# 29 blocks of seven products in a decoder layer's down projection, with sums of weights also made beside the down runs and in the output projection

## The chip, the core and the metric

One core of a Trainium2 chip runs one launch of the kernel. A core has TensorE (PE, matrix products into PSUM), VectorE (DVE), ScalarE (ACT), GpSimd (POOL) and SyncE (SP), which here only issues DMA transfers between DRAM and the core's SBUF. Each engine works through its own list of instructions in order, and they wait for each other on semaphores. The metric is the device time of one launch in microseconds, as a median of runs.

## What is computed

A decoder layer for 256 tokens of width 2048, in float32:

```python
h = rms_norm(x, attn_norm_g)
q, k, v, p = split(h @ w_in)                     # 1024 columns each
a = moba_attention(rms_norm(q), rms_norm(k), v, rel_bias)
m = multiscale_pool(p, pool_w, pool_scale)
x = x + concatenate([a, m]) @ w_out              # output projection, 2048 x 2048
h = rms_norm(x, ffn_norm_g)
u = causal_conv(h @ w_up)                        # up projection, 2048 x 11264
gate, val = split(u)
x = x + (silu(gate) * val) @ w_down              # down projection, 5632 x 2048
```

The change touches the down projection and what prepares it.

## The kernel before

**Three products for one.** A float32 operand is kept as a high part (rounded by ScalarE to a shorter format, `wh`) and a low part (the rest, `wl`, by VectorE). A product is the sum of three matmuls: high x high, high x low, low x high (`product`).

**Rows of weights.** All weights stream from DRAM in the order of use, as *rows* of 128 x 2048 floats (1 MB). For each row SP issues a load into a tile `raw` (`load`, L151), ScalarE makes the high part (`high`, L182), VectorE the low part (`low`, L188), TensorE multiplies. There are four `raw` tiles and, from the output projection on, a fifth; four tiles for high parts, three for low parts. They are used in turn. The low part's end releases the `raw` tile, and `release` then issues the next load of a fixed order. SP takes its loads in that order, so a load whose tile is not free yet holds up what stands behind it.

**Steps.** The program is a list of half rows, written out by one loop at the end of `layer`. At the half row u the loop writes: the high part of the row three ahead, the low part of the row two ahead, a sum of weights if one is due there (`make`), delayed work (`agenda`, filled by `later(n, f)`: n half rows on), deferred work (the folds), and then the matmuls of u. Each engine's order follows from this.

**Thirds and runs.** After the output projection the 22 hidden blocks of 256 are done in three *thirds* (8, 8 and 6 blocks). In each an up stage computes the hidden values, and then two down *runs* follow, one for each half of the 2048 output columns (`nb` 0 and 1). A run adds its blocks' products in PSUM and at its end adds that to the residual `x2`.

**Eights and sevens.** The product of a hidden block (2 tiles of tokens x 2 of hidden) with its weights (2 x 2 tiles, 512 columns wide) takes eight products: an *eight*, one row of kind "tok", 24 matmuls. A *seven* takes seven products after Strassen and Winograd, 21 matmuls, of sums of hidden tiles (`left_sums`) and sums of weight tiles. It needs two rows: a *sum* row (four tiles, among them three sums) with 12 matmuls, and a *rest* row (three tiles, 1536 columns) with 9. Which blocks of a run are sevens is told by `SEVEN`. Some of the products of a run's sevens are kept in PSUM banks of their own (`run["p"]`); after the last seven a *fold* (`seven_sums`: a copy by ScalarE, L918, and seven operations of VectorE, L919 to L926) brings them into the residual.

**Sums of weights.** The sums for a seven are made ahead, by one of two ways, and lie in DRAM (`mixed`) until their row is loaded. By `make`: the four tiles are loaded as a row, VectorE does three additions (L196 to L198), SP stores the result (L199). By `make_stage`: POOL issues four accumulating transfers. Before, 22 of the 26 are made by `make`, all in the up stages, and four by `make_stage`:

```python
SEVEN = ((1, 2, 3, 4, 5), (1, 2, 3, 4, 5), (1, 2, 3))
STAGES = (0, 2, 4, 6)
EARLY = (72, 72, 80, 80)
BY_DVE = ((2, 3, 4, 5, 6, 7), (0, 0.5, 1, 1.5, 2, 3, 4, 5, 6, 7), (0, 0.5, 1, 2, 3, 4))
```

**PSUM.** A run has eight banks of 512 columns: two pairs (`acc`, here `twos`) and four single ones (`ones_`). In the first run of a third the output gathers in the single ones (`c`) and the sevens' products in the pairs (`p`), in the second the other way round.

Of the kernel before, what the change touches and what calls it, by code (L numbers as in the profile page):

```python
# [26 lines left out]
OP = mybir.AluOpType  # L27
# [32 lines left out]
SOFF, SPAD = 32, 64  # L60
# [8 lines left out]
def plan():  # L69

    rows = [(k, i) for i, k in enumerate(24 * ["tok"] + 25 * ["feat"])]
    makes, t = [(u, None) for u in EARLY], 0
    for (g0, g1), sevens, by_dma, by_dve in zip(THIRDS, SEVEN, BY_DMA, BY_DVE):
        c = rows[-1][1] + 1
        makes += [(2 * c + u, None) for u in by_dma] + [(None, len(rows) + 4 * int(p) + (5 if p % 1 else 2)) for p in by_dve]
        rows += [("feat", c + i) for i in range(4 * (g1 - g0))]
        c = rows[-1][1] + 1
        for i in range(2 * (g1 - g0)):
            if i % (g1 - g0) in sevens:
                rows.append(("sum", t))  # L80
                t += 1
            rows.append(("rest" if i % (g1 - g0) in sevens else "tok", c + i))
    assert len(makes) == t, (len(makes), t)
    return rows, makes
# [12 lines left out]
def layer(ctx: ExitStack, tc: tile.TileContext, xT, wts, mix, mix12, par, rel_d, ident_d, icnt_d, out):  # L97
# [28 lines left out]
    order = [r for c in range(len(rows)) for r in [c] + [("make", i) for i, m in enumerate(makes) if m[1] == c]][4:]  # L126
# [74 lines left out]

    def make_stage(i, stage):

        t = mixed[i].rearrange("p (a n) -> p a n", n=512)
        if stage == 0:
            nc.gpsimd.dma_start(mixed[i], mix[i])
        elif stage == 1:
            nc.gpsimd.dma_start(t[:, :2], mix12[i][:, None, :].to_broadcast([P, 2, 512]), accum_op=OP.add)
        elif stage == 2:
            nc.gpsimd.dma_start(t[:, 2], t[:, 0], accum_op=OP.add)  # L210
        else:
            nc.gpsimd.dma_start(t[:, 3], t[:, 2], accum_op=OP.add)
# [391 lines left out]
    hold, splits, now, agenda, pending = set(), [], [0], {}, []  # L604
# [92 lines left out]
    def open_late():  # L697
        ectx.close()
        pool = ctx.enter_context(tc.tile_pool(name="late", bufs=1))
        late["pool"] = pool  # L700
        late["x2f"] = [block("x2f").rearrange("p (k t) -> p k t", t=S) for _ in range(4)]
# [13 lines left out]
    def block(name, dt=F32):  # L715
        return late["pool"].tile([P, SPAD + 1024], dt, name=name, tag="sums", bufs=5)[:, SOFF:SOFF + 1024]
# [39 lines left out]
    def sums2():  # L756
        sq, pool = late["sq"], late["pool"]
        x, r = sq[:, 1, :], pool.tile([P, 8], F32, name="prow", tag="prow")
        nc.vector.transpose(x, sq[:, 0, :])
        nc.vector.tensor_reduce(r, x.rearrange("p (j b) -> p j b", b=32), axis=AX.X, op=OP.add)  # L760
        q = pool.tile([32, 3, 8], F32, name="qrow", tag="qrow")
# [7 lines left out]
        late["row"] = pool.tile([P, S], F32, name="row", tag="row")  # L769
        nc.gpsimd.dma_start(late["row"], bass.AP(tensor=d.tensor, offset=d.offset, ap=[[0, P], [1, S]]))  # L770
# [92 lines left out]
    def left_sums(y):  # L863

        y = y.rearrange("p a (b n) -> p (a b) n", n=P)
        a11, a21, a12 = (y[:, i, :] for i in range(3))
        s = late["pool"].tile([P, 2, S], F32, name="ls", tag="ls").rearrange("p a (b n) -> p (a b) n", n=P)
        nc.vector.tensor_tensor(s[:, :2, :], y[:, 0:4:3, :], y[:, 1:2, :].to_broadcast([P, 2, P]), op=OP.subtract)
        nc.vector.tensor_tensor(s[:, 2, :], s[:, 1, :], a11, op=OP.add)
        nc.vector.tensor_tensor(s[:, 3, :], a12, s[:, 2, :], op=OP.subtract)  # L870
# [14 lines left out]
    def seven_mixed(u, j, run, first):  # L885

        c = where[u][0]
        t3, t1, t2, t4 = quarters(c)
        del wparts[c]
        s3, s1, s2 = (tuple(late["S", j][:, a, i, :] for a in range(2)) for i in range(3))  # L890
        a22 = tuple(late["hid"][:, 2 * j + 1, a, P:] for a in range(2))
        p1, p5, p6, p7 = run["p"]
        product(p5, s1, t1, first, False)
        product(p6, s2, t2, first, False)
        product(p7, s3, t3, first, False)
        product(run["c"][1][0], a22, t4, (1, 0) in run["left"], False)

    def seven_rest(u, j, run, first, last):
# [5 lines left out]
        s4 = tuple(late["S", j][:, a, 3, :] for a in range(2))  # L904
# [5 lines left out]
        if last:  # L910
            deferred.append(lambda: seven_sums(run))

    def seven_sums(run):

        x2, c = late["x2"], run["x2"]
        p1, p5, p6, p7 = run.pop("p")
        a, b, d = (scratch(n).rearrange("p a n -> p (a n)") for n in ("sa", "sb", "sa"))
        nc.scalar.activation(a, p1, AF.Copy)  # L918
        nc.vector.tensor_tensor(b, a, p6, op=OP.subtract)  # L919
# [6 lines left out]
        nc.vector.tensor_tensor(second, second, p5[:, None, :].to_broadcast([P, 2, 512]), op=OP.subtract)  # L926

# [25 lines left out]
    for n, ((g0, g1), sevens) in enumerate(zip(THIRDS, SEVEN)):  # L953
        ups = []
        for g in range(g0, g1):
            ups.append(feat_block(lambda: late["h"], XK, lambda ps, g=g: gate(ps, g)))
            ups.append(feat_block(lambda: late["h"], XK,
                                  lambda ps, g=g, j=g - g0, sevens=sevens, end=g == g1 - 1: value(ps, g, j, j in sevens, end)))
# [5 lines left out]
        for nb in range(2):  # L964
            run = {"n": nb * 1024}

            def done(t, lo, m, run=run, n=n, nb=nb):
# [10 lines left out]
                if n == 2:  # L978
                    k = min(m, 768 - lo) if nb and t else m
                    nc.sync.dma_start(out[:, t, run["n"] + lo:run["n"] + lo + k], x2[:, :k])  # L980
# [4 lines left out]
            for j in range(g1 - g0):  # L985
                def chunk(u, j=j, nb=nb, run=run, sevens=sevens, size=g1 - g0, fresh0=fresh0, end=n == 2 and nb == 1):
                    if j == 0:
# [17 lines left out]
                steps.append([lambda u, j=j, run=run, sevens=sevens: j in sevens and  # L1005
# [6 lines left out]
    for k, lag in enumerate(STAGES):  # L1012
        for i, (m, _) in enumerate(makes):
            if m is not None:
                agenda.setdefault(m + lag, []).append(lambda i=i, k=k: make_stage(i, k))
# [6 lines left out]
    for u in range(n):  # L1022
# [4 lines left out]
        elif u in starts:  # L1027
            c, now[0] = starts[u] + 2, u
            if c < FROM:
# [7 lines left out]
            for i, m in enumerate(makes):  # L1037
                if m[1] == c:
# [15 lines left out]
def chunks(w_in, pool_w, w_out, w_up, w_down):  # L1054
# [5 lines left out]
    (_, makes), mix, mix12 = plan(), [], []  # L1060

    def pair(w, k, c0, seven):
        b11, b12, b21, b22 = (w[(k + i) * P:(k + i + 1) * P, c0 + j * 512:c0 + (j + 1) * 512]
                              for i in range(2) for j in range(2))
        if seven:
            mix.append(np.concatenate([b22, *((b11, b11) if makes[len(mix)][1] is None else (b12, b11)), b21], axis=1))
            mix12.append(b12)
# [15 lines left out]
    for (g0, g1), sevens in zip(THIRDS, SEVEN):  # L1083
        for g in range(g0, g1):
            out += feat(w_up, 256 * g, XK) + feat(w_up, DFF + 256 * g, XK)
        for nb in range(2):
            for j in range(g1 - g0):
                out += pair(w_down, 2 * (g0 + j), 1024 * nb, j in sevens)
    return np.stack([np.concatenate(out[i:i + 2], axis=1) for i in range(0, len(out), 2)]), np.stack(mix), np.stack(mix12)
# [38 lines left out]
```

## Time and profile before

| | |
|---|---|
| median of 3 runs | 990.45 us (990.42 to 991.35) |
| the profiled execution | 990.44 us, its span 988.6 us |
| granted TensorE clock | 1.000 |
| TensorE, busy share of the span | 99%, 5282 matmuls |
| VectorE | 83%, 854 instructions |
| ScalarE | 62%, 719 instructions |
| GpSimd | 8%, 134 instructions |
| DMA | 285.34 MB, mean 289 GB/s |

The span runs from the first to the last instruction of one execution; the execution's own time has some 1.8 us around it. A group of instructions is printed as line, engine, operation, out<-in, partitions x elements and count, then busy time in us and the mean of one in ns, then the engine's idle time just before them and what ended it. A timeline's row has start and length in us, the engine, line and operation, and in brackets the idle time ahead of it and its releaser. Names in a row are those of the program's tiles.

### The profile page before, as it was taken

To read this page: it belongs to the slowest core of one execution; us is meant where nothing else is said; L and a number is where in the kernel's file an instruction comes from. 1 tells how busy PE (TensorE), PEld (TensorE's weight loads), DVE (VectorE), ACT (ScalarE), POOL (GpSimd) and SP (SyncE) were. 2 spreads that over 40 slices of the span, in tenths; PEclk is the share of its full clock that TensorE was granted. 3 is DMA by queue.
4 is the path that set the end of the run, shared out by engine and by line. 5 is a ranking of instruction groups with operands and counts; after the bars stand their busy time and mean duration, and the time that the engine had idled before them with its cause. 6 is when DMAs were issued, how large, how long until landed. Compare 5 with 4: busy or idle time off the path is not lost.

```text
span 988.6 us, 13485 instructions
## 1 busy us (share of the span) xinstructions
PE 983.5 (99%) x5282; PEld 851.7 (86%) x5282; DVE 816.5 (83%) x854; ACT 610.8 (62%) x719; POOL 74.6 (8%) x134
## 2 busy tenths in 40 slices
PE   9999999999999999999999999999999999999998
PEld 8888888898888888888888888888888888888887
DVE  6776859867678988998899888998888888898886
ACT  6654446456447767776755646886774646766742
POOL 0302322211112310000000000000000000000000
PEclk9999999999999999999999999999999999999999
DMA  9959775699978889676978788879687988776582
GB/s 349 317 207 305 248 242 202 208 330 367 297 206 305 275 335 351 259 294 230 390 259 336 297 338 334 343 296 341 231 313 291 380 290 336 287 305 255 191 326 79
DMA packets 49038, 285.34 MB, mean 289 GB/s; under 512 B 6712, under 2 KB 9400, under 8 KB 20496
## 3 DMA queue, kind: packets, MB, share of 16 engines
q1 hardware_dynamic: 41920, 264.17, 71.5%
q0 software_dynamic: 7056, 20.33, 7.7%
q8 instruction: 41, 0.67, 0.3%
q14 instruction: 21, 0.17, 0.0%
HBM read 253.14 MB, written 39.72 MB: 296 GB/s over the span
## 4 chain that ended last, share of the span: by engine, by line
PE 99%; DMA 0%; DVE 0%; SPq 0%; ACT 0%; issue 0%; DVEq 0%
PE ps_feat L276 41%; PE ps_down L879 22%; PE ps_feat L278 21%; PE ps_tok L264 9%; PE ps_val L254 4%; PE ps_pool L285 1%; PE ps_s L497 1%; DMA raw<-in_wts 0%; PE ps_av L533 0%; PE ps_av L535 0%; PE ps_val L245 0%; DVE x L977 0%; SPq L151 0%; ACT wh L159 0%; PE ps_feat L273 0%; PE ps_row L409 0%
## 5 line engine op out<-in xcount | busy, mean ns | idle before, releaser
L276 PE MATMUL ps_feat<-x2h,wh 128*128 128x512 f32 x1406 | 478.2, 389 | 0.0
L188 DVE TENSOR_TENSOR wl<-raw,wh 128x2048 fp32r<-128x2048 f32 (+1 forms) x171 | 375.6, 2204 | 25.9 <-ACT wh L182 8.0
L278 PE MATMUL ps_feat<-x2h,wl 128*128 128x256 f32 x1408 | 388.6, 276 | 0.0
L182 ACT ACTIVATE wh<-raw 128x2048 fp32r<-128x2048 f32 (+1 forms) x171 | 316.1, 1852 | 107.6 <-PE ps_down L879 55.9
L276 PEld LDWEIGHTS ps_feat<-x2h,wh 128*128 128x128 f32 x1406 | 263.9, 188 | 54.8
L278 PEld LDWEIGHTS ps_feat<-x2h,wl 128*128 128x128 f32 x1408 | 264.3, 188 | 0.0
L879 PE MATMUL ps_down<-wh,hid 128*128 128x512 f32 (+1 forms) x448 | 142.6, 387 | 0.0
L160 DVE TENSOR_TENSOR wl<-raw,wh 128x2048 fp32r<-128x2048 f32 (+3 forms) x44 | 82.9, 1894 | 37.7 <-ACT wh L159 29.5
L545 ACT ACTIVATE fs<-ps_feat 128x512 f32<-128x512 f32 x52 | 31.1, 598 | 133.5 <-PE ps_feat L278 117.4
L879 PEld LDWEIGHTS ps_down<-wh,hid 128*128 128x128 f32 x448 | 83.9, 188 | 17.3
L276 PE MATMUL ps_feat<-cat,wh 128*128 128x512 f32 x256 | 87.3, 389 | 0.0
L879 PE MATMUL ps_down<-wl,hid 128*128 128x512 f32 (+1 forms) x224 | 86.7, 387 | 0.0
L548 DVE TENSOR_TENSOR fs<-ps_feat,fs 128x512 f32<-128x512 f32 x52 | 35.8, 689 | 60.8 <-ACT fs L545 60.8
L264 PE MATMUL ps_tok<-wh,xh 128*128 128x512 f32 x256 | 80.1, 391 | 0.0
L813 ACT ACTIVATE z<-u,pv 128x256 f32<-128x256 f32 x176 | 79.1, 498 | 0.0
L159 ACT ACTIVATE wh<-raw 128x2048 fp32r<-128x2048 f32 (+3 forms) x44 | 69.3, 1598 | 10.5 <-DMA raw<-in_wts 7.6
L278 PE MATMUL ps_feat<-cat,wl 128*128 128x256 f32 x256 | 70.7, 276 | 0.0
L879 PE MATMUL ps_down<-wh,sums 128*128 128x512 f32 x208 | 69.2, 389 | 0.0
L819 DVE TENSOR_TENSOR y<-y,z 128x512 f32<-128x512 f32 x88 | 60.6, 688 | 9.2 <-ACT z L813 4.2
L276 PEld LDWEIGHTS ps_feat<-cat,wh 128*128 128x128 f32 x256 | 48.1, 188 | 10.0
L264 PEld LDWEIGHTS ps_tok<-wh,xh 128*128 128x128 f32 x256 | 48.1, 188 | 9.9
L811 ACT ACTIVATE y<-u,pv 128x256 f32<-128x256 f32 x88 | 51.8, 588 | 0.0
(190 smaller groups left out, 1013.7 us busy)
## 6 DMA issues: line engine op xcount, KB each, us to landing
raw<-in_wts SPq DMA_DIRECT2D x152, 1024.0 KB, 7.4
raw<-mixed SPq DMA_DIRECT2D x26, 1024.0 KB, 6.6
raw<-in_mix SPq DMA_DIRECT2D x22, 1024.0 KB, 6.8
mixed<-raw SPq DMA_DIRECT2D x22, 1024.0 KB, 6.5
raw<-in_wts SPq DMA_DIRECT2D x26, 768.0 KB, 5.5
raw<-in_wts SPq DMA_DIRECT2D x4, 512.0 KB, 7.1
mixed<-in_mix POOLq DMA_DIRECT2D x4, 512.0 KB, 16.8
mixed<-mixed POOLq DMA_DIRECT2D x8, 256.0 KB, 9.3
```

The costliest lines, as they stand in the source:

```text
L159: nc.scalar.activation(wh, w, AF.Copy)
L160: nc.vector.tensor_tensor(wl, w, wh.bitcast(F32), op=OP.subtract)
L182: nc.scalar.activation(w, raws[c][:, :width(c)], AF.Copy)
L188: nc.vector.tensor_tensor(wl, raws[c][:, :width(c)], wh.bitcast(F32), op=OP.subtract)
L254: nc.tensor.matmul(ps[b][:, t, :], xh[:, k, a, ts], w[:, ws], start=False, stop=(k == KT - 1 and n == 2), skip_group_check=True)
L264: nc.tensor.matmul(ps[:, t, :], act[:, k0 + k, a, ts], w[:, ws], start=(first and k == 0 and n == 0), stop=(last and k == 1 and n == 2))
L276: nc.tensor.matmul(ps, wh[:, ws], act[:, k, :, :], start=(bool(first) and n == 0), stop=False, skip_group_check=True)
L278: nc.tensor.matmul(ps[:, S:], wl[:, ws], act[:, k, 0, :], start=False, stop=(last and n == len(ks) - 1), skip_group_check=True)
L811: nc.scalar.activation(y[:, m, :], u[:, m, 2:], AF.Identity, scale=cw[2], bias=col(C_CB + f))
L813: nc.scalar.activation(z[i][:, m, :], u[:, m, 1 - i:1 - i + S], AF.Copy, scale=cw[1 - i])
L819: nc.vector.tensor_tensor(y, y, t, op=OP.add)
L879: nc.tensor.matmul(ps, a, w, start=(first and n == 0), stop=(last and n == 2), skip_group_check=True)
```

## The change

Five things change together.

- **More sevens.** `SEVEN` is now told per run: 5 and 5 in the first third, 6 and 6 in the second (5 and 5 before), 4 and 3 in the last (3 and 3 before): 29 in place of 26.
- **All 29 sums by VectorE.** `make_stage` and its array go. `EARLY` now names rows of the output projection (38, 40, 42, 44), behind whose low part a sum is made. 21 sums lie in the up stages. Four are made beside sevens: one in each run of the first two thirds, just behind the low part of the rest row of block 4 (`BESIDE`).
- **The fold in two parts.** ScalarE's copy is issued right behind the last seven's matmuls. VectorE does four of the seven operations then and three two half rows later (except at the program's end).
- **PSUM banks.** In the second run of a third the output gathers in one pair and two single banks, and the products in the other pair and the other single banks; in the first run the two pairs swap places.
- **The left sums** are made in place, by four operations of 128 columns in place of one of 256 and two of 128, and their low part is written out ahead of a row's low part (`firsts`). The output's stores of the first run of the last third come two half rows later. Tiles of the pool "late" are laid out anew.

```diff
-SEVEN = ((1, 2, 3, 4, 5), (1, 2, 3, 4, 5), (1, 2, 3))
-STAGES = (0, 2, 4, 6)
-EARLY = (72, 72, 80, 80)
-BY_DMA = ((), (), ())
-BY_DVE = ((2, 3, 4, 5, 6, 7), (0, 0.5, 1, 1.5, 2, 3, 4, 5, 6, 7), (0, 0.5, 1, 2, 3, 4))
+SEVEN = (2 * ((1, 2, 3, 4, 5),), 2 * ((1, 2, 3, 4, 5, 6),), ((1, 2, 3, 4), (1, 2, 3)))
+EARLY = (38, 40, 42, 44)
+PLACES = ((2, 3, 4, 5, 6, 7), (0, 0.5, 1, 1.5, 2, 3, 4, 5, 6, 7), (0, 0.5, 1, 2, 3))
+BESIDE = (4, 4, None)
...
+            if i % (g1 - g0) == beside:
+                makes.append(len(rows))
+            rows.append(("rest" if seven else "tok", c + i))
...
     def left_sums(y):
...
-        nc.vector.tensor_tensor(s[:, :2, :], y[:, 0:4:3, :], y[:, 1:2, :].to_broadcast([P, 2, P]), op=OP.subtract)
-        nc.vector.tensor_tensor(s[:, 2, :], s[:, 1, :], a11, op=OP.add)
-        nc.vector.tensor_tensor(s[:, 3, :], a12, s[:, 2, :], op=OP.subtract)
+        for out_, a, b, op in ((3, 3, 1, OP.subtract), (1, 0, 1, OP.subtract), (0, 3, 0, OP.add), (2, 2, 0, OP.subtract)):
+            nc.vector.tensor_tensor(s[:, out_, :], s[:, a, :], s[:, b, :], op=op)
         pending.append(lambda: nc.scalar.activation(parts[:, 0], s, AF.Copy))
-        later(4, lambda: nc.vector.tensor_tensor(parts[:, 1], s, parts[:, 0].bitcast(F32), op=OP.subtract))
+        firsts.setdefault(now[0] + 4, []).append(
+            lambda: nc.vector.tensor_tensor(parts[:, 1], s, parts[:, 0].bitcast(F32), op=OP.subtract))
...
         if last:
-            deferred.append(lambda: seven_sums(run))
+            a = scratch("sa").rearrange("p a n -> p (a n)")
+            nc.scalar.activation(a, run["p"][0], AF.Copy)
+            deferred.append(lambda: seven_sums(run, a))
...
-    def seven_sums(run):
+    def seven_sums(run, a):
...
         nc.vector.tensor_tensor(c(0, 0), a, c(0, 0), op=OP.add)
-        nc.vector.tensor_tensor(c(0, 1), c(0, 1), b, op=OP.subtract)
+        d = scratch("sd").rearrange("p a n -> p (a n)")
         nc.vector.tensor_tensor(d, b, p7, op=OP.add)
-        nc.vector.tensor_tensor(c(1, 0), d, c(1, 0), op=OP.add)
-        nc.vector.tensor_tensor(c(1, 1), c(1, 1), d, op=OP.subtract)
         second = x2[:, :, run["n"] + 512:run["n"] + 1024]
         nc.vector.tensor_tensor(second, second, p5[:, None, :].to_broadcast([P, 2, 512]), op=OP.subtract)
+
+        def rest():
+            nc.vector.tensor_tensor(c(0, 1), c(0, 1), b, op=OP.subtract)
+            nc.vector.tensor_tensor(c(1, 0), d, c(1, 0), op=OP.add)
+            nc.vector.tensor_tensor(c(1, 1), c(1, 1), d, op=OP.subtract)
+        if run["end"]:
+            rest()
+        else:
+            later(2, rest)
...
-                        run["c"], run["acc"], p = (twos, pair, ones_) if nb else (ones_, (None, None), twos)
-                        if end:
-                            run["c"], run["acc"], p = [twos[0], ones_[0]], (pair[0], None), [twos[1], ones_[1]]
-                        run["p"] = p[1][1], p[0][0], p[0][1], p[1][0]
-                        run["spare"] = p[1][1]
+                        if nb:
+                            run["c"], run["acc"], p = [twos[1], ones_[0]], (pair[1], None), [twos[0], ones_[1]]
+                        else:
+                            run["c"], run["acc"], p = ones_, (None, None), twos[::-1]
+                        run["p"] = p[0][0], p[1][1], p[0][1], p[1][0]
+                        run["spare"] = p[0][0]
```

What it moves is seen best in the engines' own lists. VectorE in the first run of the second third, from the rest row of block 4 on, before (1536 wide is a rest row, 2048 a sum row or an eight; L919 begins the fold):

```order
L188 TENSOR_TENSOR wl<-raw,wh 128x1536
L188 TENSOR_TENSOR wl<-raw,wh 128x2048
L188 TENSOR_TENSOR wl<-raw,wh 128x1536
L188 TENSOR_TENSOR wl<-raw,wh 128x2048 x3
L919 TENSOR_TENSOR sb<-sa,ps_down 128x512
L920 TENSOR_TENSOR x_2569<-sa,x_2569 128x512
```

And after, from the same row on:

```order
L189 TENSOR_TENSOR wl<-raw,wh 128x1536
L197 TENSOR_TENSOR raw<-raw 128x1024
L198 TENSOR_TENSOR raw<-raw 128x512
L199 TENSOR_TENSOR raw<-raw 128x512
L189 TENSOR_TENSOR wl<-raw,wh 128x2048
L189 TENSOR_TENSOR wl<-raw,wh 128x1536
L189 TENSOR_TENSOR wl<-raw,wh 128x2048
L189 TENSOR_TENSOR wl<-raw,wh 128x1536
L189 TENSOR_TENSOR wl<-raw,wh 128x2048 x2
L908 TENSOR_TENSOR sb<-sa,ps_down 128x512
L909 TENSOR_TENSOR x_2580<-sa,x_2580 128x512
```

The sum's three additions stand between the rest row of block 4 and the sum row of block 5; block 6 has a sum row and a rest row of its own, and one eight less precedes the fold.

SP's loads and stores of the same run, from the sum row of block 4 on, before (`mixed` are sum rows, `in_wts` all others):

```order
L151 DMA raw<-mixed_88 128x2048
L151 DMA raw<-in_wts 128x1536
L151 DMA raw<-mixed_89 128x2048
L151 DMA raw<-in_wts 128x1536
L151 DMA raw<-in_wts 128x2048 x3
L151 DMA raw<-mixed_90 128x2048
```

And after (`in_mix` is the load for a sum to be made, `mixed_97<-raw` its store):

```order
L152 DMA raw<-mixed_88 128x2048
L152 DMA raw<-in_wts 128x1536
L152 DMA raw<-in_mix 128x2048
L152 DMA raw<-mixed_89 128x2048
L152 DMA raw<-in_wts 128x1536
L152 DMA raw<-mixed_90 128x2048
L152 DMA raw<-in_wts 128x1536
L200 DMA mixed_97<-raw 128x2048
L152 DMA raw<-in_wts 128x2048 x2
L152 DMA raw<-mixed_91 128x2048
```

The load and the store of the sum, and the two rows of block 6, now stand ahead of the load of the run's last eight, which is the first of the last two `in_wts` rows.

More of the change, by code (lines that the diff above doesn't have):

```diff
@@ L71, in plan @@
     rows = [(k, i) for i, k in enumerate(24 * ["tok"] + 25 * ["feat"])]
-    makes, t = [(u, None) for u in EARLY], 0
-    for (g0, g1), sevens, by_dma, by_dve in zip(THIRDS, SEVEN, BY_DMA, BY_DVE):
+    makes, t = list(EARLY), 0
+    for (g0, g1), sevens, places, beside in zip(THIRDS, SEVEN, PLACES, BESIDE):
         c = rows[-1][1] + 1
-        makes += [(2 * c + u, None) for u in by_dma] + [(None, len(rows) + 4 * int(p) + (5 if p % 1 else 2)) for p in by_dve]
+        makes += [len(rows) + 4 * int(p) + (5 if p % 1 else 2) for p in places]
         rows += [("feat", c + i) for i in range(4 * (g1 - g0))]
@@ L78, in plan @@
         for i in range(2 * (g1 - g0)):
-            if i % (g1 - g0) in sevens:
+            seven = i % (g1 - g0) in sevens[i // (g1 - g0)]
+            if seven:
                 rows.append(("sum", t))
                 t += 1
-            rows.append(("rest" if i % (g1 - g0) in sevens else "tok", c + i))
+            if i % (g1 - g0) == beside:
+                makes.append(len(rows))
+            rows.append(("rest" if seven else "tok", c + i))
     assert len(makes) == t, (len(makes), t)
@@ L96, in layer @@
 @with_exitstack
-def layer(ctx: ExitStack, tc: tile.TileContext, xT, wts, mix, mix12, par, rel_d, ident_d, icnt_d, out):
+def layer(ctx: ExitStack, tc: tile.TileContext, xT, wts, mix, par, rel_d, ident_d, icnt_d, out):
     nc = tc.nc
@@ L125, in layer @@
     mixed = [dram.tile([P, CH], F32, name=f"mixed{i}", tag=f"mixed{i}") for i in range(len(makes))]
-    order = [r for c in range(len(rows)) for r in [c] + [("make", i) for i, m in enumerate(makes) if m[1] == c]][4:]
+    order = [r for c in range(len(rows)) for r in [c] + [("make", i) for i, m in enumerate(makes) if m == c]][4:]
     def width(c):
@@ L200, in make @@
         later(2, load_next)
[L202 to L212, printed above, removed]
     def half(u):
@@ L700, in open_late @@
         late["pool"] = pool
+        late["prow"] = pool.tile([P, 8], F32, name="prow", tag="prow")
+        late["qrow"] = pool.tile([32, 3, 8], F32, name="qrow", tag="qrow")
         late["x2f"] = [block("x2f").rearrange("p (k t) -> p k t", t=S) for _ in range(4)]
@@ L715, in block @@
     def block(name, dt=F32):
-        return late["pool"].tile([P, SPAD + 1024], dt, name=name, tag="sums", bufs=5)[:, SOFF:SOFF + 1024]
+        return late["pool"].tile([P, 1024], dt, name=name, tag="sums", bufs=6)
     def residual(ps, g):
@@ L757, in sums2 @@
         sq, pool = late["sq"], late["pool"]
-        x, r = sq[:, 1, :], pool.tile([P, 8], F32, name="prow", tag="prow")
+        x, r, q = sq[:, 1, :], late["prow"], late["qrow"]
         nc.vector.transpose(x, sq[:, 0, :])
         nc.vector.tensor_reduce(r, x.rearrange("p (j b) -> p j b", b=32), axis=AX.X, op=OP.add)
-        q = pool.tile([32, 3, 8], F32, name="qrow", tag="qrow")
         for i in range(3):
@@ L768, in sums2 @@
         nc.gpsimd.dma_start(d, q[:, 0, :])
-        late["row"] = pool.tile([P, S], F32, name="row", tag="row")
+        late["row"] = pool.tile([P, 2, S], F32, name="row", tag="y0")[:, 0, :]
         nc.gpsimd.dma_start(late["row"], bass.AP(tensor=d.tensor, offset=d.offset, ap=[[0, P], [1, S]]))
@@ L889, in seven_mixed @@
         del wparts[c]
-        s3, s1, s2 = (tuple(late["S", j][:, a, i, :] for a in range(2)) for i in range(3))
+        s2, s3, _, s1 = (tuple(late["S", j][:, a, i, :] for a in range(2)) for i in range(4))
         a22 = tuple(late["hid"][:, 2 * j + 1, a, P:] for a in range(2))
@@ L903, in seven_rest @@
         a11, a12 = (tuple(late["hid"][:, 2 * j + k, a, :P] for a in range(2)) for k in range(2))
-        s4 = tuple(late["S", j][:, a, 3, :] for a in range(2))
+        s4 = tuple(late["S", j][:, a, 2, :] for a in range(2))
         c0 = run["c"][0]
@@ L957, in layer @@
             ups.append(feat_block(lambda: late["h"], XK,
-                                  lambda ps, g=g, j=g - g0, sevens=sevens, end=g == g1 - 1: value(ps, g, j, j in sevens, end)))
+                                  lambda ps, g=g, j=g - g0, sevens=sevens, end=g == g1 - 1: value(ps, g, j, j in sevens[0], end)))
         u0 = len(steps)
@@ L964, in layer @@
         for nb in range(2):
-            run = {"n": nb * 1024}
+            run = {"n": nb * 1024, "end": n == 2 and nb == 1}
             def done(t, lo, m, run=run, n=n, nb=nb):
@@ L979, in done @@
                     k = min(m, 768 - lo) if nb and t else m
-                    nc.sync.dma_start(out[:, t, run["n"] + lo:run["n"] + lo + k], x2[:, :k])
+                    store = lambda: nc.sync.dma_start(out[:, t, run["n"] + lo:run["n"] + lo + k], x2[:, :k])
+                    store() if nb else later(2, store)
             run["done"] = done
@@ L985, in layer, with chunk @@
             for j in range(g1 - g0):
-                def chunk(u, j=j, nb=nb, run=run, sevens=sevens, size=g1 - g0, fresh0=fresh0, end=n == 2 and nb == 1):
+                def chunk(u, j=j, nb=nb, run=run, sevens=sevens[nb], size=g1 - g0, fresh0=fresh0, end=n == 2 and nb == 1):
                     if j == 0:
@@ L1004, in layer @@
                 steps.append([chunk])
-                steps.append([lambda u, j=j, run=run, sevens=sevens: j in sevens and
+                steps.append([lambda u, j=j, run=run, sevens=sevens[nb]: j in sevens and
                               seven_rest(u, j, run, j == sevens[0], j == sevens[-1])])
@@ L1028, in layer @@
             c, now[0] = starts[u] + 2, u
+            for f in firsts.pop(u, ()):
+                f()
             if c < FROM:
@@ L1087, in chunks @@
             for j in range(g1 - g0):
-                out += pair(w_down, 2 * (g0 + j), 1024 * nb, j in sevens)
-    return np.stack([np.concatenate(out[i:i + 2], axis=1) for i in range(0, len(out), 2)]), np.stack(mix), np.stack(mix12)
+                out += pair(w_down, 2 * (g0 + j), 1024 * nb, j in sevens[nb])
+    return np.stack([np.concatenate(out[i:i + 2], axis=1) for i in range(0, len(out), 2)]), np.stack(mix)
 def kernel(x, attn_norm_g, w_in, q_norm_g, k_norm_g, rel_bias, pool_w, pool_scale,
```

26 lines of the change are left out of this document (8 added, 18 removed).

## The prediction

> **What bounds the kernel now.** I read the page's head and chain first, then the waits of PE, then the groups by form, and last the timelines around one border between two down runs.
>
> ```profile
> span 988.6 us, 13485 instructions
> PE 983.5 (99%) x5282; PEld 851.7 (86%) x5282; DVE 816.5 (83%) x854; ACT 610.8 (62%) x719; POOL 74.6 (8%) x134
> PE 99%; DMA 0%; DVE 0%; SPq 0%; ACT 0%; issue 0%; DVEq 0%
> PE ps_start L328 <- DVE ones L316: 1.1, 1, 1.1
> PE ps_val L245 <- ACT wh L159: 0.3, 1, 0.3
> ```
>
> TensorE is busy for 983.5 of 988.6 us, the chain that ended last is TensorE's, and its two listed waits, 1.4 us together, lie at the start. So a matmul that goes is gained in full, **as long as nothing else gets late**. VectorE has 172 us free, but over the whole span; what counts is where the change puts its work.
>
> ```profile
> 458.33 80.26 PE ps_down L879 x354
> 712.72 80.26 PE ps_down L879 x354
> ```
>
> These pieces of the chain are the two runs of the first and of the second third, without a break: 80.26/354 = 0.2267 us per matmul, 5.44 for a block as eight (24), 4.76 for a seven (21).
>
> **Matmuls.** Sevens go from 26 to 29, each three matmuls fewer: third 0 keeps 5+5, third 1 goes from 5+5 to 6+6, third 2 from 3+3 to 4+3. That is 9 x 0.2267 = **−2.04 us**. The sum below starts from the profiled execution's own 990.44, which is the median (990.45) to 0.01.
>
> **What a sum of weights costs.**
>
> ```profile
> L188 DVE TENSOR_TENSOR wl<-raw,wh 128x2048 fp32r<-128x2048 f32 x145 | 330.9, 2285 | 21.7 <-ACT wh L182 8.0 <-issue 5.4 <-ACT z L813 3.1
> L188 DVE TENSOR_TENSOR wl<-raw,wh 128x1536 fp32r<-128x1536 f32 x26 | 45.6, 1753 | 4.2 <-PE ps_down L879 4.2
> L196 DVE TENSOR_TENSOR raw<-raw 128x1024 f32<-128x1024 f32 x22 | 26.8, 1218 | 1.0 <-DMA raw<-in_mix 1.0
> L197 DVE TENSOR_TENSOR raw<-raw 128x512 f32<-128x512 f32 x22 | 15.2, 692 | 0.8
> L198 DVE TENSOR_TENSOR raw<-raw 128x512 f32<-128x512 f32 x22 | 15.2, 692 | 0.7
> L182 ACT ACTIVATE wh<-raw 128x2048 fp32r<-128x2048 f32 x145 | 278.0, 1917 | 90.5 <-PE ps_down L879 42.8 <-DMA raw<-in_wts 31.8 <-PE ps_feat L276 9.0
> ```
>
> One sum is 1.218 + 0.692 + 0.692 = 2.60 us of VectorE, a load of 1 MB and a store of 1 MB. 22 are made so now; seven more will be. Nothing of this is on the chain, so each is worth only what it delays.
>
> ```profile
> 213.00:257.00 44.00, 30.13 (x30) 1.00 1.04 344
> 713.00:752.00 39.00, 34.62 (x28) 1.00 0.78 300
> ```
>
> *Four in the output projection* (first row: window, VectorE's busy time, clock, DMA share, GB/s): 30.13 + 4 x 2.60 = 40.5 of 44.0 us. It fits, one sum per two rows. I take 0. The lower end is 0 too, as TensorE waits for nothing there; the upper end is one sum ahead of a low part that is just due, 2.6.
>
> *POOL's sums go.*
>
> ```profile
> mixed<-in_mix POOLq DMA_DIRECT2D x4, 512.0 KB, 16.8
> mixed<-raw SPq DMA_DIRECT2D x22, 1024.0 KB, 6.5
> ```
>
> The POOL transfers give way to four loads and four stores on SP's queue in the same stretch; POOL's busy share is 8% and no wait of TensorE names it: 0.
>
> *One sum in each run of thirds 0 and 1, behind the low part of the rest row of block 4.* In the second row above the run has 34.62 of 39.0 us busy. A sum (2.60), and in third 1 one more rest row for block 6 (1.75), make 38.97, while the run shrinks by 0.68 to 38.3. So **VectorE is overfull there**, unless it started ahead. Row by row in the first run of third 1:
>
> ```profile
> 722.83 11.88 DVE L188 TENSOR_TENSOR wl<-raw,wh 128x1536 fp32r<-128x1536 f32 x6
> 735.05 1.76 DVE L188 TENSOR_TENSOR wl<-raw,wh 128x1536 fp32r<-128x1536 f32 x1 [0.34 <-PE ps_down L879]
> 737.74 4.73 DVE L188 TENSOR_TENSOR wl<-raw,wh 128x2048 fp32r<-128x2048 f32 x2 [0.93 <-ACT wh L182]
> ```
>
> The six are rest and sum rows in turn, the last the sum row of block 5; so the low part of rest 4 ends at 722.83 + 11.88 − 2.29 = 732.4. The new sum holds VectorE to 735.0, the sum row of block 5 to 737.3. TensorE wants that row at 712.72 + 108 x 0.2267 = 737.2: **0.1 late**, so in four runs **+0.4**. Rest 5 then ends at 739.05 (before: 736.81).
>
> *The closing block (block 7, an eight).* In the changed program its load goes into the tile that rest 5 leaves, so SP issues it at 739.1. Before, it was one of the four loads that the second row here holds:
>
> ```profile
> 724.61 0.32 SPq L151 DMA_DIRECT2D raw<-mixed  x1
> 726.81 5.87 SPq L151 DMA_DIRECT2D raw<-in_wts  x4
> 734.74 0.33 SPq L151 DMA_DIRECT2D raw<-mixed  x1
> ...
> 735.79 1.92 ACT L182 ACTIVATE wh<-raw 128x2048 fp32r<-128x2048 f32 x1 [1.79 <-DMA raw<-in_wts]
> 738.23 1.92 ACT L182 ACTIVATE wh<-raw 128x2048 fp32r<-128x2048 f32 x1 [0.52 <-DMA raw<-in_wts]
> 740.71 1.92 ACT L182 ACTIVATE wh<-raw 128x2048 fp32r<-128x2048 f32 x1 [0.57 <-DMA raw<-in_wts]
> 743.15 1.92 ACT L182 ACTIVATE wh<-raw 128x2048 fp32r<-128x2048 f32 x1 [0.52 <-DMA raw<-mixed]
> ```
>
> The second row of ACT (738.23) is that block today. All four end a wait for a transfer, 2.46 us apart: the loads stand in a queue here, 1 MB in 2.46 us. The change puts ahead of the block the sum's load (1 MB), its store (1 MB), and 1.75 MB for block 6 in place of 1: 2.75 MB more, 2.75 x 2.46 = 6.8, so it lands at about 738.2 + 6.8 = 745.0. Two rows from the landings bound it:
>
> ```profile
> DMA to landing us min/median/max: 4.8/4.8/4.8
> ...
> DMA to landing us min/median/max: 8.3/8.3/8.3
> ```
>
> The first is a 1 MB load with the queue to itself (issued at 539.4), the second the one issued at 734.7. From 739.1 they give 743.9 and 747.4; the queue's 745.0 stands nearer to the first. ACT's 1.92 and VectorE's 2.29 follow: ready at 749.2. TensorE wants it at 712.72 + 150 x 0.2267 = 746.7, plus the 0.1 above: **late by 2.4** (1.4 by the first row, 4.8 by the second). The second run has the same pattern: **2 x 2.4 = +4.8**. Third 0 has no block 6; its closing loads move by a sum's transfer and the next queue place, and slack of about 2 us holds them: 0, at most 0.3 in each run.
>
> [...]
>
> *Folding in two parts, and the PSUM banks.*
>
> ```profile
> 745.58 0.69 DVE L919 TENSOR_TENSOR sb<-sa,ps_down 128x512 f32<-128x512 f32 x1 [0.62 <-ACT sa L918]
> ...
> 749.43 1.22 DVE L926 TENSOR_TENSOR x<-x,ps_down 128x1024 f32<-128x1024 f32 x1
> 750.57 1.28 DVE L977 TENSOR_TENSOR x<-ps_down,x 128x512 f32<-128x512 f32 x2
> ```
>
> Today seven operations fold a run, 4.99 us up to 750.57. They stay seven; three move two rows later. In third 1 the fold now waits for a copy on ACT that stands behind the high part of the next run's first sum row. That row's load comes two places behind the closing block: 745.0 + 2 x 2.46 = 749.9, high part to 751.8, copy to 752.3. From there by starts: first part 2.97, half of the output 1.20, low part 2.20, other half 1.20, rest row 1.67, three folds 1.83, low part of the second sum row 2.29: ready at 765.7. TensorE, with 2.5 of stalls, wants it at 712.72 + 2.5 + 219 x 0.2267 = 764.9: **0.8 late**. It is 0 if that load comes 0.8 sooner, and 1.4 if VectorE's operations don't overlap as their starts do today. In third 0 the half of the output that ends before the second run's sevens has about 2 us, and the fold starts 1 to 2 us later: 0. The swapped PSUM banks cost something only where a product starts before the fold has read its bank, and that place is in the 0.8.
>
> *The rest.*
>
> ```profile
> L868 DVE TENSOR_TENSOR ls<-y 128x256 f32<-128x256 f32 x13 | 5.4, 418 | 0.0
> L870 DVE TENSOR_TENSOR ls<-y,ls 128x128 f32<-128x128 f32 x13 | 3.8, 292 | 0.4
> ```
>
> Left sums become four operations of 128 columns in place of one of 256 and two of 128: 4 x 0.292 for 1.002, 0.17 more in each of 15 blocks (13 before). The up stages hide it: they lose one of their 22 sums (2.60 each) and TensorE waits for nothing there; without that cover it would be 15 x 0.17 = 2.5 at most. The stores of third 2's first run go out two rows later, with the whole second run still to come: 0, and with no cover a store's 6.5 once, which only the last stores can cost. Third 2 gets no sum beside, so its runs keep the loads of today; its one more seven costs VectorE 1.75: 0, or at worst a 0.1 as above.
>
> **Sum:** −2.04 + 4.8 + 0.4 + 0.8 = +3.96; 990.44 + 3.96 = **994.4 us**.
>
> **Rivals.**
>
> *Slack covers everything*: −2.04 gives 988.4, faster. It decides if block 7 lands by 746.7 − 2.29 − 1.92 = 742.5, 3.4 us after its issue, or, with a lone landing of 4.8, if rest 5 leaves its tile by 737.7 and not at 739.1. For it: VectorE idles 21.7 us before its low parts over the whole kernel, so it may come into the run ahead. Against: no load above took under 4.8, and the six low parts of 722.83 already run without idle time.
>
> *A lone landing*: both stalls 1.4, the fold in time: 2.8 + 0.4 − 2.04 = +1.2, 991.6, no change that shows. For it: the window of the run has a DMA share of 0.78 only.
>
> *A full queue*, 8.3 us per landing, for which the row issued at 734.7 speaks, and against which the three ahead of it do, which came 2.46 apart: 9.6 + 0.4 + 0.8 − 2.04 = +8.8, 999.2, and up to 2.4 more if the fold's row slips by as much again: 1001.6.
>
> *The clock falls back after a stall.* The program's start shows what that costs:
>
> ```profile
> 1.06 3.78 PE L328 MATMUL ps_start<-ones 128*128 128x128 f32 x16 [1.06 <-DVE ones L316]
> 4.50 1.20 PE L245 MATMUL ps_val<-wh,xh 128*128 128x256 f32 x4
> ...
> 5.91 0.71 PE L245 MATMUL ps_val<-wh,xh 128*128 128x256 f32 x4
> ```
>
> Four matmuls of one shape take 1.20 us at 4.50 and 0.71 at 5.91: from 1.06 to 5.91 TensorE ran at about half pace, 2.4 us lost. Two stalls that bring this on add 4.8: 999.2. Against: no stall in this trace is followed by it, as there is none behind the start. [...]
>
> *The change doesn't do what it says*: a sum in the output projection holds up a low part there, 2.6 at most beside the rest: 997.0.
>
> **How the numbers follow.** About 0.2% (988.47 to 992.43) is what a measurement of this kernel can tell from no change. Slack covers everything 0.08; lone landing 0.25; forecast 0.48, its own range 992.0 to 998.0, of which 0.03 count as no change; full queue 0.12; clock 0.04; output projection 0.03. Faster 0.08, same 0.28, slower 0.64. A range of 989.0 to 1000.0 leaves out the first rival, half of the full queue and part of the clock's, under 0.2.
>
> **What would show it.** Right: TensorE's waits list the closing eights of third 1, for VectorE's low part behind ACT's high part behind a load, 1.4 to 4.8 us each; small waits at the sum rows of block 5; none in the output projection. The down chain of third 1 has 348 matmuls and lasts longer than 80.26 us. Wrong: its chain lasts 348 x 0.2267 = 78.9 us, or the load of block 7 is issued well before 739, or the largest wait names another row.

## The result, and the profile after

The changed kernel takes 1002.92 us (median of 5 runs, 1000.02 to 1003.24) against 990.46 us before: a ratio of 1.0115, with a 95% interval of 1.0101 to 1.0130. It is slower, as forecast, but by 12.5 us where 4.0 were forecast, and outside the range given (989.0 to 1000.0). The profiled execution took 1003.24 us. Of all executions in this document one, of the run with the transfers alone, took 3056.74 us; it is left out of that run's ratio but not of its median (the other three: 1000.90 to 1002.69).

The page's head and the start of its chain, and the waits of TensorE (line waited on, releaser: us in total, times, longest):

```profile
span 1001.5 us, 13517 instructions
PE 987.4 (99%) x5273; PEld 851.2 (85%) x5273; DVE 843.7 (84%) x903; ACT 615.7 (61%) x724; POOL 60.9 (6%) x118
PE 40%; DMA 4%; DVE 3%; ACT 1%; issue 1%; ACTq 0%; DVEq 0%
PE ps_down L867 <- DVE wl L189: 5.7, 5, 1.8
PE ps_down L867 <- DVE x L973: 1.8, 2, 1.1
PE ps_down L867 <- ACT wh L183: 0.9, 2, 0.6
```

There are nine matmuls fewer, as intended (5282 to 5273). But the chain that ended last (followed back to 506 us only, so its shares don't add up to 100%), all TensorE before, now runs through DMA, VectorE and ScalarE too, and three groups of waits at the down products (L867) have appeared. Busy time hides a part of it: TensorE is busy 3.9 us longer with fewer matmuls.

The first run of the second third, which the prediction worked out row by row, starts here at 716.27 (712.56 before, by its first matmul; the 3.7 us between were lost in the first third). ScalarE's timeline, and with it VectorE's, from the sum onwards:

```profile
738.02 3.32 ACT L183 ACTIVATE wh<-raw 128x2048 fp32r<-128x2048 f32 x2 [5.05 <-DMA raw<-mixed]
742.85 3.45 ACT L183 ACTIVATE wh<-raw 128x2048 fp32r<-128x2048 f32 x2 [1.51 <-DMA raw<-mixed]
750.27 1.92 ACT L183 ACTIVATE wh<-raw 128x2048 fp32r<-128x2048 f32 x1 [3.97 <-DMA raw<-in_wts]
...
736.47 1.22 DVE L197 TENSOR_TENSOR raw<-raw 128x1024 f32<-128x1024 f32 x1
739.97 3.96 DVE L189 TENSOR_TENSOR wl<-raw,wh 128x2048 fp32r<-128x2048 f32 x2 [0.83 <-ACT wh L183]
752.22 2.29 DVE L189 TENSOR_TENSOR wl<-raw,wh 128x2048 fp32r<-128x2048 f32 x1 [3.46 <-ACT wh L183]
```

Behind the sum (736.47) VectorE waits for ScalarE, and ScalarE for transfers, by up to 5.05 us. The row of 738.02 is the sum row of block 5, the row of 750.27 the closing block. SP issued the latter's load at 743.96:

```profile
739.17 0.33 SPq L200 DMA_DIRECT2D mixed<-raw  x1
743.96 0.80 SPq L152 DMA_DIRECT2D raw<-in_wts  x2
```

One window of TensorE (busy time, matmuls, granted clock, DMA share, GB/s) has what no list of waits has:

```profile
755.00:759.00 4.00, 4.00 (x13) 0.60 1.02 410
```

It is busy throughout, at a granted clock of 0.60. TensorE's timeline ahead of that window shows the waits themselves, and in it one matmul per 0.427 us in place of 0.227:

```profile
752.24 0.50 PE L867 MATMUL ps_down<-wh,hid 128*128 128x512 f32 x1 [0.27 <-ACT wh L183]
754.57 0.50 PE L867 MATMUL ps_down<-wl,hid 128*128 128x512 f32 x1 [1.82 <-DVE wl L189]
...
757.54 0.63 PE L867 MATMUL ps_down<-wl,hid 128*128 128x512 f32 x1
757.96 1.06 PE L867 MATMUL ps_down<-wh,hid 128*128 128x512 f32 x2
```

Measured from start to start, less 0.227 us a matmul, the lost time is:

| place | forecast | measured |
|---|---|---|
| nine matmuls fewer | −2.0 | −2.0 |
| sum rows of block 5, four runs | 0.4 | 0.0 + 0.9 + 1.4 + 0.6 = 2.9 |
| closing eights of the second third | 4.8 | 2.6 + 3.0 = 5.6 |
| border of the two runs, second third | 0.8 | 0 |
| border of the two runs, first third, and an eight there | 0 | 2.3 + 0.3 = 2.6 |
| half pace behind the two closing eights | a rival | 1.6 + 1.7 = 3.3 |
| sum | +4.0 | +12.4 |

The profiled executions differ by 12.8. The rest doesn't lie at the start, for the first down run starts at 458.2 us in both; it is spread in pieces too small to list over the same runs, with 0.2 us behind the last matmul.

### The profile page after: what moved, and what is told of

It is laid out like the page before. It is cut to its first block, busy times and chain, and to the rows that moved or that the text cites. A ratio compares the mean times of both kernels' runs of the same rounds, so it can differ in the third digit from the quotient of the medians.

```text
span 1001.5 us, 13517 instructions
## 1 busy us (share of the span) xinstructions
PE 987.4 (99%) x5273; PEld 851.2 (85%) x5273; DVE 843.7 (84%) x903; ACT 615.7 (61%) x724; POOL 60.9 (6%) x118
## 5 line engine op out<-in xcount | busy, mean ns | idle before, releaser
L189 DVE TENSOR_TENSOR wl<-raw,wh 128x2048 fp32r<-128x2048 f32 (+1 forms) x174 | 379.6, 2195 | 33.6 <-ACT wh L183 27.2
L183 ACT ACTIVATE wh<-raw 128x2048 fp32r<-128x2048 f32 (+1 forms) x174 | 319.9, 1845 | 118.8 <-DMA raw<-in_wts 59.1
L867 PE MATMUL ps_down<-wh,hid 128*128 128x512 f32 (+1 forms) x418 | 136.9, 394 | 1.6 <-ACT wh L183 0.9
L867 PEld LDWEIGHTS ps_down<-wh,hid 128*128 128x128 f32 x418 | 79.7, 191 | 19.5 <-ACT wh L183 1.7
L867 PE MATMUL ps_down<-wl,hid 128*128 128x512 f32 (+1 forms) x209 | 82.5, 395 | 3.6 <-DVE wl L189 3.6
L867 PE MATMUL ps_down<-wh,sums 128*128 128x512 f32 x232 | 77.3, 390 | 1.1 <-DVE x L973 1.1
```

The costliest lines, as they stand in the source:

```text
L183: nc.scalar.activation(w, raws[c][:, :width(c)], AF.Copy)
L189: nc.vector.tensor_tensor(wl, raws[c][:, :width(c)], wh.bitcast(F32), op=OP.subtract)
L867: nc.tensor.matmul(ps, a, w, start=(first and n == 0), stop=(last and n == 2), skip_group_check=True)
```

## The experiments

The time of the kernel before beside these runs was 990.5 to 990.6 us throughout.

**Take the four sums beside sevens away.**

```diff
-                makes.append(len(rows))
+                makes.append(None)
```

Their four rows are then loaded from `mix`, unsummed.

> The changed kernel without the four sums beside sevens: no load, no additions and no store for them there. Their four sum rows are loaded as the four unsummed tiles, so the sums of weights of these four blocks are left out. Theory A (every wait of TensorE behind the start comes from these four sums): 990.4 - 2.0 = 988.4 us, and no wait at the down products. Rival B (the sixth seven of a run, the fold in two parts or the swapped banks have a price of their own): the 2.3 us at the border of the first third (1.0 and 1.3 before the second run's sevens) or part of the 5.6 us at the closing eights of the second third stay, 990.7 to 996 us.

988.64 us; ratio 0.9981 (0.9971 to 0.9990), 2.0 us under the kernel before beside it. No wait at the down products is left. So all of the 14 us lost, the half pace and the border of the first third among them, hang on the four sums, and the nine matmuls bring what they were priced at. Rival B falls.

**Which part of a sum: transfers or additions?** First the transfers alone:

```diff
-        nc.vector.tensor_tensor(r[:, :1024], r[:, :1024], r[:, 512:1536], op=OP.add)
+        if i not in BARE:
+            nc.vector.tensor_tensor(r[:, :1024], r[:, :1024], r[:, 512:1536], op=OP.add)
...
```

> The four sums beside sevens keep their load and their store; VectorE's three additions for them are left out, so these four rows of sums aren't summed. If the transfers are the cause (the sum's load stands ahead of the sum row of block 5, the store ahead of the closing block): the sum rows of block 5 and the closing eights wait as in the changed kernel, within 1 us each, 997 to 1003 us. If VectorE's 2.60 us are the cause: 988.4 to 991 us.

1002.05 us, ratio 1.0106 (1.0086 to 1.0126): as slow as the whole change. Then the additions alone:

```diff
+        if i in BARE:
+            x, y = late["x2"][:, 0, :1024], scratch("sd").rearrange("p a n -> p (a n)")
+            for k in range(4):
+                nc.vector.tensor_tensor(y, x[:, :512], x[:, 512:], op=OP.add)
+            return
```

> The four sums beside sevens keep VectorE's time only: four additions of 128x512 (4 x 0.69 us, some 2.6 us from first start to last end) on tiles that are at hand, with no load and no store. The four rows of sums are loaded unsummed, so these sums are left out. If the transfers are the cause: 988.4 to 990.5 us, with at most 0.1 us at each sum row of block 5 as the prediction worked it out. If VectorE's time is the cause: over 994 us.

990.2 us, ratio 0.9998 (0.9989 to 1.0008): 1.6 us over the run without sums. VectorE's 2.60 us are the small part; the transfers are the large one.

**Load or store?** The load alone (then the tile is given back at once):

```diff
+        if i in BARE:
+            later(2, load_next)
+            return
```

> The four sums beside sevens keep their load only; no additions, no store, and their four sum rows are loaded unsummed, so these sums are left out. If the load ahead of the sum row of block 5, and the tile that it takes, carry most: the sum rows of block 5 wait 0.5 to 1.5 us each, the border of the first third and the closing eights 1 to 2 us less than in the changed kernel: 993 to 997 us. If the store carries most: 988.4 to 991 us.

991.83 us, ratio 1.0012 (1.0003 to 1.0021): 3.2 us over the run without sums, less than expected. The store alone, taken from the residual:

```diff
+        if i in BARE:
+            nc.sync.dma_start(mixed[i], late["x2"][:, 0, :])
+            return
```

> The four sums beside sevens keep a store of 1 MB at their place (of a part of the residual that is at hand); no load, no additions, and their four sum rows are loaded unsummed, so these sums are left out. If the load carries most: 988.4 to 991 us, with waits at closing eights only. If the store carries most: 993 to 998 us.

990.91 us, ratio 1.0012 (0.9999 to 1.0026), 2.3 us over the run without sums; two of its ten executions took 996, which nothing here explains. It doesn't show what the store costs at its place in the change: with no load for the sum the queue runs one place ahead, and SP issued this store behind the closing block's load (731.37 to 733.36, then the store), so it put off the next run's rows, not the closing block.

```profile
731.37 1.99 SPq L153 DMA_DIRECT2D raw<-in_wts  x2
733.41 0.43 SPq L197 DMA_DIRECT2D mixed<-x  x1
```

The two alone, 3.2 and 2.3, don't add up to the 13.4 of both. How late the closing block's high part starts after its run's start shows why. In the first run of the second third it is 27.86 us without sums (740.59 − 712.73), 29.88 with the load (743.29 − 713.41), and with both 32.95 (transfers alone) to 34.00 (the change: 750.27 − 716.27). ScalarE's rows in the first two, and in the change the row of 750.27 above:

```profile
740.59 1.92 ACT L184 ACTIVATE wh<-raw 128x2048 fp32r<-128x2048 f32 x1 [0.99 <-DVE wl L190]
```

```profile
743.29 1.92 ACT L184 ACTIVATE wh<-raw 128x2048 fp32r<-128x2048 f32 x1 [0.96 <-DVE wl L190]
```

Without sums the closing row is ready 2.0 us before TensorE wants it. The load uses this up, and what the store adds behind it is all waiting. In the second run the load alone goes beyond it: 27.76 us without sums (779.99 − 752.23), 31.61 with the load (785.08 − 753.47), 33.35 in the change (794.89 − 761.54). So the two transfers cost 5.6 to 6.1 us together in the change, but which of them weighs more differs between the two runs.

**The tile, or the bytes?** I took the tile for the cause now: a sum holds one of five from its load's issue to its store's landing, and so the closing block must take the tile of rest 5.

```diff
+        if i in BARE:
+            nc.sync.dma_start(mixed[i], late["x2"][:, 0, :])
+            later(2, load_next)
+            return
```

> The four sums beside sevens keep a load and a store of 1 MB each at their places, as in the run with transfers only (1002.05 us), but the store is taken from the residual, so the tile that the sum was loaded into is free again once it has landed; no additions, and the four sum rows are loaded unsummed, so these sums are left out. Theory: the tile, held from the load's issue to the store's landing, makes the closing block's load wait for the tile of rest 5 (issued at 743.3 there, at 733.7 in the run with the load only). With it free: that load is issued before 736, the closing eights and the border of the first third wait 1 us at most each, 991.5 to 995 us. Rival (the bytes in the queue): 999 to 1003 us as with transfers only.

1002.23 us, ratio 1.0107 (1.0090 to 1.0123). This theory fell, and clearly: SP issued the closing block's load 7.4 us earlier than in the change, and it was ready for ScalarE only 0.7 us earlier.

```profile
735.27 0.70 SPq L198 DMA_DIRECT2D mixed<-x  x1
736.56 5.57 SPq L153 DMA_DIRECT2D raw<-in_wts  x2
...
749.55 1.92 ACT L184 ACTIVATE wh<-raw 128x2048 fp32r<-128x2048 f32 x1 [3.84 <-DMA raw<-in_wts]
```

Issued at 736.56 (its place is the first of the two), high part at 749.55: 13 us in a full queue. The windows of the change show the queue (the last two numbers are DMA share and GB/s):

```profile
717.00:730.00 13.00, 13.00 (x59) 10.68 (x58) 11.39 (x11) 11.06 (x15) 0.00 (x0) 1.00 0.48 167
730.00:756.00 26.00, 22.77 (x98) 17.88 (x97) 20.60 (x13) 14.31 (x9) 0.00 (x0) 1.00 0.97 380
```

The early part of the run leaves the queue half empty, since tiles aren't free (SP issues the sum's load at 728.84, when the low part that ends at 728.81 gives its tile back), and the part with the sum is full to 0.97.

**Half the bytes.**

```diff
+        n = HALF if isinstance(c, tuple) and c[1] in BARE else n
...
+            nc.sync.dma_start(mixed[i][:, :HALF], late["x2"][:, 0, :HALF])
```

> As the run with the tile freed (1002.23 us), with the load and the store of the four sums beside sevens cut to their first 512 KB; no additions, and their four sum rows are loaded unsummed, so these sums are left out. If the bytes ahead of the closing block's load set its landing (1 MB of load put it off by 2.0 us, 1 MB of store by 3.4): it comes 2.7 us earlier than there, within 1 us of what TensorE needs, no half pace, 990 to 993.5 us. If the number of transfers and their places set it: 999 to 1003 us.

995.18 us, ratio 1.0043 (1.0026 to 1.0060): between the two expectations, and 7 us less than with full size. In the first run of the second third the closing block comes 1.9 us earlier (31.45 after the run's start, 33.30 with full size) where 2.7 were expected; in the second run it comes 1.4 us later (34.62, 33.23 with full size). Of the 5.3 us between the two profiled executions (996.79 and 1002.05) 3.2 are half pace, which no wait of this run is followed by (granted clock 1.000 here, 0.996 there). So bytes matter, but half of them took only some 2 us off the waits themselves; how much of a transfer's cost is its place in the queue stays open.

**Make the four sums in an up stage.** Ten in the first third's stage:

```diff
-PLACES = ((2, 3, 4, 5, 6, 7), (0, 0.5, 1, 1.5, 2, 3, 4, 5, 6, 7), (0, 0.5, 1, 2, 3))
+PLACES = ((2, 2.5, 3, 3.5, 4, 4.5, 5, 5.5, 6, 7), (0, 0.5, 1, 1.5, 2, 3, 4, 5, 6, 7), (0, 0.5, 1, 2, 3))
+BESIDE = (None, None, None)
```

> The changed kernel with the four sums made in the up stage of the first third in place of beside sevens (ten there in place of six); all is computed. Theory A: 988.4 us, no wait at the down products. Rival (the up stage of the first third is overfull with ten sums: VectorE 170.99 us busy of 201 before, and 4 x 2.60 more, and four times 2 MB more on the queue in the same stretch): waits of 0.5 to 2 us at some rows there, 989 to 993 us.

993.67 us, ratio 1.0036 (1.0025 to 1.0046), with two listed waits of 0.9 us in the first third: the rival. The trace is that of its fastest execution (992.08 us, granted clock 1.000), so these waits don't show all of the median's 5.0 us over the run without sums; seven of the ten executions, up to 997.38 us, had a granted clock of 0.997 or 0.998, so half pace may have a part in it, which is not shown. Spread over two stages it goes:

```diff
+PLACES = ((2, 3, 3.5, 4, 5, 5.5, 6, 7), (0, 0.5, 1, 1.5, 2, 3, 4, 5, 6, 7), (0, 0.5, 1, 2, 3, 4, 5))
+BESIDE = (None, None, None)
```

> The changed kernel with the four sums spread over up stages: eight in the first third's (six in the changed kernel), ten in the second's as there, seven in the last third's (five there); none beside sevens; all is computed. If a crowd of sums in one stage was what the run with ten sums in the first third's stage waited for: 988.4 to 988.8 us and no wait at the products. If any further sum in an up stage costs: 989.5 to 993 us.

**988.65 us, ratio 0.9980 (0.9971 to 0.9989)**, with all computed and no wait at the products: this version is faster than both, and as fast as the one whose four sums were left out.

**The fold, and one seven more,** both on that version.

```diff
-        if run["end"]:
+        if True:
             rest()
```

> The version with the sums spread over up stages (988.65 us), with the fold's seven operations of VectorE in one piece again; all is computed. If the fold in two parts is needed for the second runs: the three operations come 1.8 us sooner and put off the half of the output that ends before the second run's sevens; 0.5 to 1.5 us at each of two borders, 989.5 to 991.5 us. If the border has that room without the sums beside: 988.4 to 988.9 us.

990.26 us, ratio 0.9996 (0.9987 to 1.0005): 1.6 us over the version with the fold in two parts. One listed wait stands for most of it, in the last third, where the half of the output that ends late holds TensorE:

```profile
PE ps_down L867 <- DVE x L973: 1.0, 1, 1.0
```

> The version with the sums spread (988.65 us) with 4 sevens in both runs of the last third, 30 in all, and one more sum in the last third's up stage; all is computed. Three matmuls fewer: 988.65 - 0.68 = 987.97 us if the last fold, now one block closer to the end, lies beside the last eight. If it does not: the fold's 4.4 us come partly behind the last matmul, 989 to 992 us.

991.36 us, ratio 1.0007 (0.9999 to 1.0016). The last matmul starts at 983.49 here and at 982.66 without the thirtieth seven, in spite of three matmuls fewer (a wait of 1.0 us for a low part in the last run), and the span goes on 5.8 us behind it instead of 3.9. So the second expectation came, the last fold partly behind the last matmul, and a wait besides.

**When does TensorE fall to half pace?** Three runs of the kernel before, one execution each, with VectorE repeating low parts so that TensorE has to wait at five rows each:

```diff
+        for n in AGAIN.get(c, ()):
+            nc.vector.tensor_tensor(wl[:, :n], raws[c][:, :n], wh[:, :n].bitcast(F32), op=OP.subtract)
```

> The kernel before, with VectorE repeating a low part at five rows of up stages (the same values written again), so that TensorE waits there: rows 61, 73, 127, 173 and 185 by 2.0, 2.5, 2.8, 3.6 and 4.4 us, worked out as the repeats' time (2.20 us full, 0.61 us a quarter) less the time that each row's low part is early in the trace of before. Theory A (the clock falls after idle time of some 2.5 us, as at both closing eights of the second third in the changed kernel): half pace after four or all five of them, some 1.6 us each: 990.4 + 15.3 + 6.6 = 1012 us. [...]

1019.52 us. The waits came out longer than planned, 2.55, 2.87, 3.55, 4.15 and 4.45 us (from start to start, less one matmul), and half pace followed all five (granted clock 0.990).

> As the run with stalls of 2.5 to 4.5 us, all of which were followed by half pace, but with shorter ones: by that run's rows 1.9, 2.2, 2.3, 2.0 and 2.0 us idle at rows 61, 73, 127, 173 and 185. Theory A (a fixed point between 2.1 and 2.5 us, since 2.1 us at one closing eight of the run with transfers only was not followed by half pace): one or two of the five at most, those above 2.1. [...]

1009.29 us. The waits were of 1.34, 1.82, 1.82, 1.86 and 1.86 us: none was followed by it (granted clock 0.999).

> The kernel before with repeated low parts, as the two runs with stalls, now for idle times of about 2.0 to 2.4 us at rows 61, 73, 127, 173 and 185. If there is a point between 2.1 and 2.4 us (2.1 us not followed by half pace, 0.3 + 2.1 us close together followed by it): half pace behind the longer ones alone. If it depends on chance: half pace behind some, not in the order of length.

1009.03 us, granted clock 0.997. The waits were of 2.42, 2.58, 2.69, 2.55 and 2.72 us. Half pace followed the first and the third alone. The first three waits end in these windows, one in each (busy time of TensorE, matmuls, granted clock, DMA share, GB/s):

```profile
351.00:357.00 6.00, 4.97 (x20) 0.72 0.69 210
421.00:427.00 6.00, 5.38 (x30) 1.00 0.67 202
658.00:664.00 6.00, 5.28 (x22) 0.72 0.61 198
```

2.42 us was followed by it and 2.58 was not: between 2.4 and 2.7 us it isn't the length alone that decides. What does is not shown. In the change the granted clock was 0.50 twice, each time behind the wait at a closing eight:

```profile
755.82:759.23 3.41, 3.41 (x9) 0.50 1.00 401
800.19:803.60 3.41, 3.41 (x9) 0.50 1.01 428
```

Ahead of both stand a wait of 2.1 us (752.24 to 754.57 by starts, and 796.86 to 799.19, less a matmul each) and, one matmul before it, a shorter one. It differs between executions too: of the five executions of the change one has a granted clock of 1.000 and took 1000.02 us, the others 0.996 or 0.997 and 1001.49 to 1003.24.

## Why the prediction was wrong

**Right:** the direction, and its main mechanism. The closing eights of the second third wait for VectorE's low part behind ScalarE's high part behind a load, twice, as forecast, and no wait appeared in the output projection. The matmuls were priced rightly (988.64 us without the sums beside). The end of POOL's sums, the later stores of the last third and the new left sums cost nothing that shows.

**Wrong, first: the sum row of block 5 (0.4 forecast, 2.9 measured).** "The new sum holds VectorE to 735.0, the sum row of block 5 to 737.3" followed VectorE alone. The load for the sum stands ahead of that row's own load in SP's order, and this the prediction counted for the closing block only. In the change ScalarE waits 5.05 us for this row, and VectorE is idle for 0.83 us behind the sum. The additions alone cost 1.6 us in all four runs, the load alone 3.2.

**Wrong, second: the border of the first third (0 forecast, 2.6 with the eight ahead of it).** "The fold starts 1 to 2 us later: 0" was the forecast. It started 4.2 us later (496.63, 492.45 before). ScalarE's copy for it stands behind the high part of the next run's first block, the row whose load comes behind the sum's store; the fold's last three operations then stand ahead of the output's half. This chain was worked out for the second third, where it gave 0.8 and came to nothing, and not for the first.

```profile
492.47 1.92 ACT L183 ACTIVATE wh<-raw 128x2048 fp32r<-128x2048 f32 x1 [4.43 <-DMA raw<-in_wts]
494.29 0.58 ACT L900 ACTIVATE sa<-ps_down 128x512 f32<-128x512 f32 x1
...
496.63 0.68 DVE L908 TENSOR_TENSOR sb<-sa,ps_down 128x512 f32<-128x512 f32 x1
```

**Wrong, third: the clock, a rival at 0.04.** Two stalls that bring half pace on were priced at 2.4 us each; they took 1.6 and 1.7. The price was fair, the chance was not. It was the author's estimate for waits of 2.4 us, and no run shows a length that parts the waits with half pace behind them from those without. What the runs show is this: waits of 2.5 and 2.8 us, each broken by one matmul, were followed by half pace in the change, and so were three of the six of 2.4 to 2.8 us in the runs with stalls.

**Off in size only: the closing eights (4.8 forecast, 5.6 measured).** "2.75 MB more, 2.75 x 2.46 = 6.8": from the run's start to the block's high part, the measured difference is 34.0 − 25.7 (738.23 − 712.56 before) = 8.3 us, and 8.6 in the second run. The block's load went out when rest 5 had left its tile, as forecast, but 27.7 us behind the run's start (743.96) where 26.4 were forecast. The sum's two transfers make 6.1 and 5.6 us of the difference, where 2 x 2.46 = 4.9 had been counted. The wait itself grew less, since TensorE came late already by the row of block 5.

The range failed with the three together: the one execution of the change without half pace took 1000.02 us, just at the range's upper end. Each had been looked at as a place with its own room. But one queue feeds all of them, and once it was full (a DMA share of 0.97 from 730 to 756 us) every later row came late by the same transfers.

## What to carry to other kernels

A piece of work that is put in beside a full engine is priced by all it asks for: its transfers stand ahead of every later load of the queue, and may cost far more than its instructions (13.4 us with the transfers alone, 1.6 with the additions alone, both over the run without sums). Room that is there for each of two additions (2.0 us here) isn't there for both; so price their sum against it, not each by itself. A forecast wait of 2.4 us or so may bring half pace behind it: three of six waits between 2.4 and 2.8 us did here, and behind the closing eights of the change it cost 1.6 and 1.7 us. So price it as a case with a chance of its own.

## What was not expected of the hardware

In the change TensorE ran at half pace twice for 3.41 us (755.82 to 759.23 and 800.19 to 803.60, granted clock 0.50). The first time it began 3.4 us behind the start of a wait of 2.1 us, the second time 3.1. It shows in the trace as matmuls 0.427 us apart at a busy share of 1: waits listed for TensorE don't contain it. Waits of nearly the same length may or may not bring it on: of six waits between 2.4 and 2.8 us in the runs with stalls three did, while the five of 1.34 to 1.86 us did not. The store of 1 MB took 8.1 us to land in the full queue, and the load of 1 MB issued at 736.56, with the tile freed early, some 13.
